# Attention layers of a hybrid backbone: the softmax division moved from the probabilities to the output, four value products to a PSUM bank

## The chip, the cores and the metric

The kernel runs on one core of one Trainium2 chip. The metric is the device time of one execution in microseconds (us); the time of a kernel is the median of its runs. A profile is one execution recorded by the hardware profiler. Its engines are PE (matrix unit; PEld is its weight load), DVE (vector), ACT (scalar), POOL (GpSimd) and SP, which issues the loads.

## The reference

Four layers work on 256 context tokens and 256 latent tokens of width 1024. Layers 0 and 3 mix tokens with windowed grouped-query attention (16 heads of 64, 4 key heads, a learned sink logit for each head; called the window layers here), layer 1 with multi-head latent attention (16 heads; the latent layer), layer 2 with a recurrence. A gated MLP follows each. What the change touches is the end of the attention:

```python
def attend(q, k, v, mask=None, sink=None):
    s = jnp.einsum("bqhgd,bkhd->bhgqk", q, k, preferred_element_type=jnp.float32) * (q.shape[-1] ** -0.5)
    if mask is not None:
        s = jnp.where(mask, s, NEG_INF)
    m = jnp.max(s, axis=-1)
    if sink is not None:
        sk = jnp.broadcast_to(sink.astype(jnp.float32)[None, :, :, None], m.shape)
        m = jnp.maximum(m, sk)
    p = jnp.exp(s - m[..., None])
    denom = jnp.sum(p, axis=-1)
    if sink is not None:
        denom = denom + jnp.exp(sk - m)
    o = jnp.einsum("bhgqk,bkhd->bqhgd", p, v.astype(jnp.float32))
    o = o / jnp.transpose(denom, (0, 3, 1, 2))[..., None]
    return o.astype(v.dtype)
```

The quotient may be taken before or after the product with v: the denominator belongs to a query row.

## The kernel before, in words

Activations lie transposed, 128 features to a tile. A weight unit of 128 x 1024 values is loaded by SP, rounded by ACT (`whi`, L214), and the rest of the rounding is taken by POOL (`wlo`, L215); a projection is three products of high and low parts (`mm3`, L224 to L226). The order of instructions on each engine is fixed when the program is built, by a scheduler that walks the program and fills an engine's gaps with later work; at run time each engine takes its own list in order.

A window layer (`swa`) projects keys, then queries, and then calls `core(p, b, j)` for one pair of heads and one block of 128 queries at a time: p is the half of the heads, b the query block (0 and 1 context, 2 and 3 latent), j the pair. Layer 0 makes 2 x 4 x 4 = 32 such calls, layer 3 (latent only) 2 x 2 x 4 = 16. In a call PE makes the scores into a bank of `mm` (L642, L643). For context DVE takes the maximum (L658 to L660), for latent a fused mask, scale and maximum (L669) and a sign change (L672). ACT takes the exponential with its row sum (L662, L673). Then the sink is added to the sum (DVE L675, ACT L676, DVE L677), the reciprocal taken (DVE L678), and the two halves of P are multiplied by it, one on DVE (L683), one on ACT (L681). PE transposes the scaled P (L691), ACT and DVE copy it (`pt`, L242, L244), PE multiplies it with v into a bank of `mo` (L697), and ACT and DVE write the result as high and low part into `o` (`split`, L258, L259), 128 columns at a time.

The latent layer (`mla`) does the same in `core(hg, hp, b)`, 4 x 2 x 4 = 32 calls, with scores L884, maximum L888 to L892, exponential L894, reciprocal L895, both scalings on DVE (L897), transposes L905 and value products L911. Between its calls the keys and queries of the next group of heads are prepared (`kv_put` and `q_mm`; transposes L834 and L858, which follow a chain of small DVE operations, L265 to L275 and `rqs`, L866).

PSUM pools have two banks each: `mm`, `fl`, `mo`, `tp`. In layer 0 the modulation vectors of the layer are computed alongside (`mod0_steps`, L339): one `mo` bank is held for a sum over 8 and then one over 16 weight tiles, one tile per call of `core`, so through most of layer 0 the attention has the other `mo` bank alone. While the second half of the heads is worked on, the output projection of the first half (`half_proj`, on `o`) is put between the calls; that of the second half (`out_tail`) follows the last call. In the window layers `o[p]` is read by these projections in four slices of j, in the latent layer in slices of (hg, hp).

## Time and profile before

| what | value |
|---|---|
| runs | 2292.27, 2292.8, 2296.81 us; median 2292.8 us |
| profiled execution, its own time | 2288.72 us |
| span of its profile, first to last instruction | 2286.9 us |
| busy: PE, DVE, ACT, POOL | 93%, 71%, 45%, 42% of the span |
| mean granted TensorE clock | 0.979 |
| chain that ended last | PE 73%, DVE 19%, ACT 4% |

The attention of layer 0 lies at about 97 to 275 us of the span, that of layer 1 at 733 to 922, that of layer 3 at 1985 to 2075. "Busy" of PE is the union of its matmuls' spans, so work that fills gaps between matmuls and work that runs back to back look alike in it. The list of waits gives, for each instruction that made its engine idle, what ended the wait. Where an engine's own list is in order, a late instruction delays all that stands behind it.

### The profile page before, as it was taken

The numbers are of one execution on the slowest core, as the hardware profiler recorded it, in microseconds if no ns is written. First come the engines' busy times: TensorE is split into PE (matmuls) and PEld (weight loads), VectorE is DVE, ScalarE is ACT, GpSimd is POOL, SyncE is SP. The second block draws the span as 40 slices with busy tenths as digits, with TensorE's granted clock in tenths as the row PEclk, the third lists the DMA queues.
The fourth block names the chain that finished last, engine by engine and source line by source line (L and its number), as shares of the span: only waits on it lengthen the run. The fifth ranks groups of instructions, "written<-read, shape, count | busy, mean of one in ns | idle before, by whom it ended". The sixth has DMA issues, their size and how long they took to land.

```text
span 2286.9 us, 32497 instructions
## 1 busy us (share of the span) xinstructions
PE 2133.3 (93%) x12084; PEld 1772.5 (78%) x12084; DVE 1628.4 (71%) x3342; ACT 1031.6 (45%) x1850; POOL 956.4 (42%) x418
## 2 busy tenths in 40 slices
PE   6989999999989998899999988899999999898999
PEld 5656788888877666888888876688888887677999
DVE  4678779777776887687879789857964457885333
ACT  4466553232246775433232356635333224575544
POOL 3231145454533002354545433344544443414887
PEclk9999999999999999999999998899999999999999
DMA  8433135555522001155556422223655552303555
GB/s 301 183 120 130 38 119 190 173 172 166 176 88 66 21 29 56 54 196 175 174 175 186 128 71 68 74 83 111 193 182 172 174 162 83 102 32 98 185 184 157
DMA packets 83884, 300.11 MB, mean 131 GB/s; under 512 B 11152, under 2 KB 12816, under 8 KB 81296
## 3 DMA queue, kind: packets, MB, share of 16 engines
q1 hardware_dynamic: 83728, 298.05, 40.2%
q8 instruction: 95, 1.56, 0.3%
q14 instruction: 61, 0.50, 0.1%
HBM read 296.97 MB, written 1.05 MB: 130 GB/s over the span
## 4 chain that ended last, share of the span: by engine, by line
PE 73%; DVE 19%; ACT 4%; issue 2%; DMA 2%; POOL 1%; SPq 0%; ACTq 0%; DVEq 0%; POOLq 0%
PE fl L225 8%; PE fl L226 8%; PE fl L224 8%; PE mm L224 7%; PE mm L226 7%; PE mm L225 7%; PE mo L225 4%; PE mo L224 4%; PE mo L226 4%; PE tp L226 2%; PE tp L224 2%; PE tp L225 2%; PE mo L697 2%; PE tp L691 2%; PE mm L884 2%
## 5 line engine op out<-in xcount | busy, mean ns | idle before, releaser
L215 POOL TENSOR_TENSOR wlo<-raw,whi 128x1024 fp32r<-128x1024 f32 (+3 forms) x367 | 922.4, 2516 | 1247.9 <-ACT whi L214 1212.4
L214 ACT ACTIVATE whi<-raw 128x1024 fp32r<-128x1024 f32 (+3 forms) x367 | 382.4, 1043 | 480.6 <-PE tp L225 189.9
L373 DVE SCALAR_TENSOR_TENSOR junk<-mw,cbc 128x1024 bf16<-128x1024 f32 x256 | 456.6, 1784 | 24.1 <-DMA mw<-in_modw_dram 15.8
L224 PE MATMUL fl<-h_hi,whi 128*128 128x512 f32 (+1 forms) x832 | 298.7, 360 | 10.4 <-DVE lam L958 5.9
L226 PE MATMUL fl<-h_hi,wlo 128*128 128x512 f32 (+1 forms) x832 | 298.9, 360 | 3.6 <-POOL wlo L215 3.6
L225 PE MATMUL fl<-h_lo,whi 128*128 128x512 f32 (+1 forms) x832 | 298.9, 360 | 0.4 <-POOL h_lo L439 0.2
L224 PE MATMUL mm<-h_hi,whi 128*128 128x512 f32 (+1 forms) x768 | 271.1, 353 | 3.1 <-ACT h_hi L435 2.7
L226 PE MATMUL mm<-h_hi,wlo 128*128 128x512 f32 (+1 forms) x768 | 270.1, 352 | 3.7 <-POOL wlo L215 3.7
L225 PE MATMUL mm<-h_lo,whi 128*128 128x512 f32 (+1 forms) x768 | 269.6, 352 | 0.8 <-POOL h_lo L439 0.2
L1109 DVE SCALAR_TENSOR_TENSOR conv<-mm,colt,conv 128x510 f32<-128x510 f32 (+1 forms) x88 | 59.8, 680 | 190.3 <-ACT conv L1107 190.3
L224 PEld LDWEIGHTS fl<-h_hi,whi 128*128 128x128 f32 x832 | 158.8, 192 | 34.2 <-issue 6.0
L1113 ACT ACTIVATE conv<-conv 128x512 f32<-128x512 f32 (+1 forms) x88 | 51.0, 580 | 287.4 <-DVE conv L1111 287.3
L226 PEld LDWEIGHTS fl<-h_hi,wlo 128*128 128x128 f32 x832 | 159.0, 191 | 27.2 <-POOL wlo L215 4.6
L225 PEld LDWEIGHTS fl<-h_lo,whi 128*128 128x128 f32 x832 | 159.1, 191 | 23.5 <-POOL h_lo L439 0.6
L224 PE MATMUL mo<-g_hi,whi 128*128 128x256 f32 (+1 forms) x488 | 165.4, 339 | 9.8 <-DVE x L449 6.8
L224 PEld LDWEIGHTS mm<-h_hi,whi 128*128 128x128 f32 x768 | 147.2, 192 | 23.3 <-ACT h_hi L435 3.7
L225 PE MATMUL mo<-g_lo,whi 128*128 128x256 f32 (+1 forms) x488 | 164.6, 337 | 0.4 <-DVE g_lo L259 0.4
L226 PEld LDWEIGHTS mm<-h_hi,wlo 128*128 128x128 f32 x768 | 146.8, 191 | 23.1 <-POOL wlo L215 4.3
L226 PE MATMUL mo<-g_hi,wlo 128*128 128x256 f32 (+1 forms) x488 | 164.4, 337 | 0.0
L225 PEld LDWEIGHTS mm<-h_lo,whi 128*128 128x128 f32 x768 | 146.3, 191 | 20.7 <-POOL h_lo L439 1.4
L449 DVE SCALAR_TENSOR_TENSOR x<-mo,modc,x 128x256 f32<-128x256 f32 x212 | 95.3, 477 | 84.2 <-PE mo L226 83.9
L224 PEld LDWEIGHTS mo<-g_hi,whi 128*128 128x128 f32 x488 | 93.1, 191 | 21.9 <-DVE x L449 7.5
(313 smaller groups left out, 4443.9 us busy)
## 6 DMA issues: line engine op xcount, KB each, us to landing
raw<-in_W_dram SPq DMA_DIRECT2D x352, 512.0 KB, 3.6
mw<-in_modw_dram SPq DMA_DIRECT2D x144, 512.0 KB, 4.2
mw<-in_modwa_dram SPq DMA_DIRECT2D x8, 1024.0 KB, 15.2
mw<-in_modwb_dram SPq DMA_DIRECT2D x16, 512.0 KB, 4.5
mw<-in_modwb_dram SPq DMA_DIRECT2D x8, 1024.0 KB, 8.6
cbc<-in_cc_dram SPq DMA_DIRECT2D x3, 1024.0 KB, 6.1
raw<-in_W_dram SPq DMA_DIRECT2D x8, 384.0 KB, 2.9
x<-in_xT_dram SPq DMA_DIRECT2D x8, 256.0 KB, 4.9
```

The source lines that it names most:

```text
L214: nc.scalar.activation(hi, raw, AF.Copy)
L215: nc.gpsimd.tensor_tensor(lo, raw, f32(hi), op=ALU.subtract)
L224: nc.tensor.matmul(ps, ah, bh, start=start and i == 0, stop=False, **kw)
L225: nc.tensor.matmul(ps, ah, bl, start=False, stop=False, **kw)
L226: op = nc.tensor.matmul(ps, al, bh, start=False, stop=stop and i == n - 1, **kw)
L373: nc.vector.scalar_tensor_tensor(junk, raw, 1.0, cbc[:, s], op0=ALU.mult, op1=ALU.mult, accum_out=modc[l][:, s, m:m + 1])
L449: nc.vector.scalar_tensor_tensor(X[m][:, half], ps[:, half], modc[l][:, s, part + m:part + m + 1], X[m][:, half], op0=ALU.mult, op1=ALU.add)
L691: nc.tensor.transpose(pp[:, c:c + 128], P[z][:, (2 * kp + kk) * 128:(2 * kp + kk + 1) * 128], ident)
L697: nc.tensor.matmul(po[r], v[0][:, kb, p * 128 + 64 * z:p * 128 + 64 * z + 64], pt[:, kp, (kk * 2 + z) * 128:(kk * 2 + z + 1) * 128], start ...
L884: nc.tensor.matmul(ps[:, c], d["q"][:96, 2 * hp + z, bc], d["k"][:96, 2 * hp + z, :nk], start=True, stop=True)
L1109: op = nc.vector.scalar_tensor_tensor(y3[:, :, 1:], g3[:, :, :255], cw[:, l, 0, f:f + 1], y3[:, :, 1:], op0=ALU.mult, op1=ALU.add)
L1113: nc.scalar.activation(y[:, t0:], y[:, t0:], AF.Silu)
```

## The change

A helper `divide` is new. Instead of scaling P, the kernel keeps the sums of the exponentials of four calls (the four j of a window layer's (p, b); the four b of a latent layer's (hg, hp)), collects the four value products in one bank of `mo`, and after the fourth takes the reciprocals of all eight sums at once, spreads them over 512 columns (ACT, `rw`), transposes that (PE, four transposes into `tp`), copies it (ACT, `rs`), multiplies the bank by it in place (DVE), and splits all 512 columns into `o`. In the window layers the latent scale `rqs` carries a minus sign, so that the fused operation gives the negated maximum at once and the sign change (L672) falls away; the sink terms are taken for eight columns at a time.

```diff
@@ -258,6 +258,19 @@
         nc.scalar.activation(hi, src, AF.Copy)
         nc.vector.tensor_tensor(lo, src, f32(hi), op=ALU.subtract)
 
+    def divide(po, rd, dst):
+        wide = tmp("rw")
+        nc.scalar.activation(wide.rearrange("p (m z d) -> p m z d", m=4, z=2),
+                             rd.rearrange("p m (z o) -> p m z o", o=1).to_broadcast([128, 4, 2, 64]), AF.Copy)
+        rb = tp_ps()
+        for m in range(4):
+            nc.tensor.transpose(rb[:, m * 128:(m + 1) * 128], wide[:, m * 128:(m + 1) * 128], ident)
+        rs = tmp("rs")
+        nc.scalar.activation(rs, rb, AF.Copy)
+        nc.vector.tensor_tensor(po, po, rs, op=ALU.mult)
+        view = po.rearrange("p (m q) -> p m q", m=4) if len(dst[0].shape) == 3 else po
+        split(dst[0], dst[1], view)
+
     def rsqrt(v, n, steps=3):
         i = small(n, "rs_i", I32)
         y = small(n, "rs_y")
@@ -634,7 +647,7 @@
                 else:
                     nc.vector.tensor_copy(qb[:, z], pq)
             rq = mean_rsqrt(ss, 8, 64)
-            nc.vector.tensor_scalar(rqs[p][:, b * 8:(b + 1) * 8], rq, 0.125, None, op0=ALU.mult)
+            nc.vector.tensor_scalar(rqs[p][:, b * 8:(b + 1) * 8], rq, 0.125 if b < 2 else -0.125, None, op0=ALU.mult)
 
         def scores(ps, p, b, j, g, nk):
             h = 2 * j + g
@@ -642,46 +655,42 @@
             nc.tensor.matmul(ps, q, kh[:, 2 * p + g, :nk], start=True, stop=False)
             nc.tensor.matmul(ps, q, kl[:, 2 * p + g, :nk], start=False, stop=True)
 
+        G = {}
+
         def core(p, b, j):
             if o[p] is None:
                 o[p] = bigs("o", 2)
+            if j == 0:
+                st = small(32, "st")
+                G[p, b] = [st[:, a * 8:(a + 1) * 8] for a in range(4)] + [mo_ps()]
+            ngm, es, den, rd, po = G[p, b]
             nk = 256 if b < 2 else 512
-            st = small(12, "st")
-            mx, ngm, es, den, rd = (st[:, a * 2:(a + 1) * 2] for a in range(5))
-            sk, nsk2 = (a.rearrange("p (k j) -> p j k", j=4)[:, j, 2 * p:2 * p + 2] for a in (snk, nsk))
+            nsk2 = nsk[:, 8 * p + j:8 * p + 8:4]
             rq2 = rqs[p][:, b * 8 + 2 * j:b * 8 + 2 * j + 2]
             P = []
             if b < 2:
                 ps, pt = mm_ps(), probs()
                 for z in range(2):
                     scores(ps[:, z * 256:(z + 1) * 256], p, b, j, z, nk)
+                mx = small(2, "mx")
                 nc.vector.tensor_reduce(mx, ps.rearrange("p (z k) -> p z k", z=2), axis=AX.X, op=ALU.max, negate=True)
                 nc.vector.tensor_tensor(mx, mx, rq2, op=ALU.mult)
-                nc.vector.tensor_tensor(ngm, mx, nsk2, op=ALU.min)
+                nc.vector.tensor_tensor(ngm[:, j::4], mx, nsk2, op=ALU.min)
                 for z in range(2):
+                    c = 4 * z + j
                     nc.scalar.activation(pt[:, z * 256:(z + 1) * 256], ps[:, z * 256:(z + 1) * 256], AF.Exp,
-                                         bias=ngm[:, z:z + 1], scale=rq2[:, z:z + 1], accum_out=den[:, z:z + 1])
+                                         bias=ngm[:, c:c + 1], scale=rq2[:, z:z + 1], accum_out=den[:, c:c + 1])
                     P.append(pt[:, z * 256:(z + 1) * 256])
             else:
                 for z in range(2):
+                    c = 4 * z + j
                     ps, pt = mm_ps(), probs()
                     scores(ps, p, b, j, z, nk)
                     nc.vector.tensor_tensor_reduce(
-                        out=pt, in0=ps, in1=mask[:, b - 2], op0=ALU.add, op1=ALU.max,
-                        scale=rq2[:, z:z + 1], scalar=sk[:, z:z + 1], accum_out=mx[:, z:z + 1])
-                    nc.vector.tensor_scalar(ngm[:, z:z + 1], mx[:, z:z + 1], -1.0, None, op0=ALU.mult)
-                    nc.scalar.activation(pt, pt, AF.Exp, bias=ngm[:, z:z + 1], accum_out=den[:, z:z + 1])
+                        out=pt, in0=ps, in1=mask[:, b - 2], op0=ALU.add, op1=ALU.min,
+                        scale=rq2[:, z:z + 1], scalar=nsk2[:, z:z + 1], accum_out=ngm[:, c:c + 1])
+                    nc.scalar.activation(pt, pt, AF.Exp, bias=ngm[:, c:c + 1], scale=-1.0, accum_out=den[:, c:c + 1])
                     P.append(pt)
-            nc.vector.tensor_tensor(es, sk, ngm, op=ALU.add)
-            nc.scalar.activation(es, es, AF.Exp)
-            nc.vector.tensor_tensor(den, den, es, op=ALU.add)
-            nc.vector.reciprocal(rd, den)
-            for z in range(2):
-                if z:
-                    nc.scalar.activation(P[z], P[z], AF.Copy, scale=rd[:, z:z + 1])
-                else:
-                    nc.vector.tensor_scalar(P[z], P[z], rd[:, z:z + 1], None, op0=ALU.mult)
-            po = mo_ps()[:, :128]
             pt = pt_p.tile([128, 2, T], F32, tag="pt", name="pt")
             for kp in range(nk // 256):
                 pp = tp_ps()
@@ -693,10 +702,15 @@
                 for kk in range(2):
                     kb = 2 * kp + kk
                     for z in range(2):
-                        r = slice(64 * z, 64 * z + 64)
-                        nc.tensor.matmul(po[r], v[0][:, kb, p * 128 + 64 * z:p * 128 + 64 * z + 64],
+                        nc.tensor.matmul(po[64 * z:64 * z + 64, j * 128:(j + 1) * 128], v[0][:, kb, p * 128 + 64 * z:p * 128 + 64 * z + 64],
                                          pt[:, kp, (kk * 2 + z) * 128:(kk * 2 + z + 1) * 128], start=kb == 0, stop=kb == nk // 128 - 1)
-            put(sel(o[p], slice(None), j, slice(b * 128, (b + 1) * 128)), po)
+            if j == 3:
+                nc.vector.tensor_tensor(es, snk[:, 8 * p:8 * p + 8], ngm, op=ALU.add)
+                nc.scalar.activation(es, es, AF.Exp)
+                nc.vector.tensor_tensor(den, den, es, op=ALU.add)
+                nc.vector.reciprocal(rd, den)
+                divide(po, rd.rearrange("p (z m) -> p m z", z=2),
+                       [t[:, :, b * 128:(b + 1) * 128] for t in o[p]])
 
         ps = {b: mm_ps() if z < 2 else fl_ps() for z, b in enumerate(range(q0, 4))}
         proj(1, ps, hook=lambda q, done: steps(mods, MQ[q]))
@@ -796,7 +810,7 @@
                     nc.vector.tensor_tensor(krg[:, b], kr, c32k[:, b - 2], op=ALU.mult)
                     nc.vector.tensor_tensor(krg[:, b], krg[:, b], r, op=ALU.add)
 
-        G, o, uq, ukv = {}, {}, {}, {}
+        G, o, uq, ukv, acc = {}, {}, {}, {}, {}
 
         def group(hg):
             G[hg] = dict(q=big("q", F32), k=big("k", F32), v=big("v", F32).rearrange("p b (c n) -> p b c n", c=2)[:, :, 0],
@@ -874,8 +888,12 @@
             nk = 512 if lat else 256
             bc = slice(b * 128, (b + 1) * 128)
             rq2 = d["rqs"][:, b * 4 + 2 * hp:b * 4 + 2 * hp + 2]
-            st = small(8, "st")
-            mx, ngm, den, rd = (st[:, a * 2:(a + 1) * 2] for a in range(4))
+            if b == 0:
+                acc[hg, hp] = small(16, "st"), mo_ps()
+            st, po = acc[hg, hp]
+            den, rd = st[:, 2 * b:2 * b + 2], st[:, 8:16]
+            st = small(4, "mx")
+            mx, ngm = st[:, 0:2], st[:, 2:4]
             P, S = [], []
             for z in range(2):
                 if z == 0 or lat:
@@ -892,10 +910,6 @@
                 nc.vector.tensor_tensor(ngm, mx, rq2, op=ALU.mult)
             for z in range(2):
                 nc.scalar.activation(P[z], S[z], AF.Exp, bias=ngm[:, z:z + 1], scale=rq2[:, z:z + 1], accum_out=den[:, z:z + 1])
-            nc.vector.reciprocal(rd, den)
-            for z in range(2):
-                nc.vector.tensor_scalar(P[z], P[z], rd[:, z:z + 1], None, op0=ALU.mult)
-            po = mo_ps()[:, :128]
             pt = pt_p.tile([128, 2, T], F32, tag="pt", name="pt")
             for kp in range(nk // 256):
                 pp = tp_ps()
@@ -908,9 +922,11 @@
                     kb = 2 * kp + kk
                     for z in range(2):
                         c = hp * 128 + 64 * z
-                        nc.tensor.matmul(po[64 * z:64 * z + 64], d["v"][:, kb, c:c + 64], pt[:, kp, (kk * 2 + z) * 128:(kk * 2 + z + 1) * 128],
+                        nc.tensor.matmul(po[64 * z:64 * z + 64, bc], d["v"][:, kb, c:c + 64], pt[:, kp, (kk * 2 + z) * 128:(kk * 2 + z + 1) * 128],
                                          start=kb == 0, stop=kb == nk // 128 - 1)
-            put(sel(o[hg // 2], slice(None), (2 * hg + hp) % 4, bc), po)
+            if b == 3:
+                nc.vector.reciprocal(rd, acc[hg, hp][0][:, 0:8])
+                divide(po, rd.rearrange("p (m z) -> p m z", z=2), [t[:, (2 * hg + hp) % 4] for t in o[hg // 2]])
 
         group(0)
         ss = small(16, "ssk")
```

How the scheduler's lists change is shown at three places.

PE, layer 0. `mo_<n>` names a bank's use and `o0_`/`o1_` the parts of `o`; rows with L642, L643 (L655, L656 in the new numbering) are scores, L691 (L700) transposes of P, L697 (L705) value products, L267 transposes of the reciprocals. Before, in the second half of layer 0, each call has its own `mo`:

```order
L697 MATMUL mo_2032<-pt_2033,v_613 64x128 x8
L691 MATMUL tp_2084<-tabt_104,P_2066 128x128 x4
L642 MATMUL mm_2200<-k_hi_653,q_1288 128x256
L643 MATMUL mm_2200<-k_lo_654,q_1288 128x256
L642 MATMUL mm_2200<-k_hi_653,q_1288 128x256
L691 MATMUL tp_2122<-tabt_104,P_2104 128x128
L224 MATMUL fl_2146<-o0_938,whi_2142 128x512
L225 MATMUL fl_2146<-o1_939,whi_2142 128x512
L697 MATMUL mo_2082<-pt_2083,v_613 64x128 x4
```

With the change, where the first group of layer 0 ends and the second begins:

```order
L705 MATMUL mo_941<-pt_1202,v_613 64x128 x4
L267 MATMUL tp_1219<-tabt_104,rw_1217 128x128 x4
L700 MATMUL tp_1248<-tabt_104,P_1236 128x128 x4
L655 MATMUL mm_1341<-k_hi_653,q_855 128x256
L656 MATMUL mm_1341<-k_lo_654,q_855 128x256
L655 MATMUL mm_1341<-k_hi_653,q_855 128x256
L656 MATMUL mm_1341<-k_lo_654,q_855 128x256
L705 MATMUL mo_1234<-pt_1247,v_613 64x128 x4
```

The four transposes of the reciprocals stand right behind the last value product of a group, and between them and the first product of the next group stand one transposed P and four scores.

PE, the end of layer 3's attention, where the last value products pass into the output projection of the second half of the heads (`o0_17456` before, `o0_17132` with the change). Before:

```order
L224 MATMUL fl_17960<-o0_17456,whi_17956 128x256
L225 MATMUL fl_17960<-o1_17457,whi_17956 128x256
L226 MATMUL fl_17960<-o0_17456,wlo_17957 128x256
L697 MATMUL mo_17916<-pt_17917,v_16670 64x128 x4
L226 MATMUL fl_17974<-o0_17456,wlo_17957 128x256
L697 MATMUL mo_17916<-pt_17917,v_16670 64x128 x4
L224 MATMUL fl_17974<-o0_17456,whi_17956 128x256
L225 MATMUL fl_17974<-o1_17457,whi_17956 128x256
L226 MATMUL fl_17974<-o0_17456,wlo_17957 128x256
```

With the change:

```order
L705 MATMUL mo_17353<-pt_17519,v_16406 64x128 x8
L267 MATMUL tp_17546<-tabt_104,rw_17544 128x128 x4
L224 MATMUL fl_17576<-o0_17132,whi_17572 128x256
L224 MATMUL fl_17590<-o0_17132,whi_17572 128x256
L225 MATMUL fl_17576<-o1_17133,whi_17572 128x256
L226 MATMUL fl_17576<-o0_17132,wlo_17573 128x256
```

Before, the projection of the earlier slices of j stands around the last value products; with the change nothing of the projection stands before the last division, since all four slices of the last block are written by it.

DVE, the last two latent calls of layer 3. Before (`st` holds the small row values, `x` is the projection's result):

```order
L669 ISA P,st<-mm,mask,rowt,rqs 128x512
L669 ISA st 128x1
L259 TENSOR_TENSOR o_17457<-mo,o_17456 128x128
L683 TENSOR_SCALAR P<-P,st 128x512
L672 TENSOR_SCALAR st<-st 128x1
L449 SCALAR_TENSOR_TENSOR x_101<-fl,modc_127,x_101 128x256
L675 TENSOR_TENSOR st<-rowt,st 128x2
L244 COPY pt<-tp 128x512
L677 TENSOR_TENSOR st<-st 128x2
L678 RECIPROCAL st<-st 128x2
L683 TENSOR_SCALAR P<-P,st 128x512
```

With the change:

```order
L689 ISA P,st<-mm,mask,nsk,rqs 128x512
L689 ISA st 128x1
L708 TENSOR_TENSOR st<-rowt,st 128x8
L710 TENSOR_TENSOR st<-st 128x8
L711 RECIPROCAL st<-st 128x8
L244 COPY pt<-tp 128x512
L462 SCALAR_TENSOR_TENSOR x_101<-fl,modc_127,x_101 128x256
L270 TENSOR_TENSOR mo<-mo,rs 128x512
L259 TENSOR_TENSOR o_17133<-mo,o_17132 128x4x128
```

Nothing of DVE stands between a latent call's exponential and its transposes any more; the sink, the reciprocal, the product (L270) and the low part follow once per group.

## Rows read from the trace of the kernel before

**Rows 1.** Busy time by stretch (start:end, us, PE, PEld, DVE, ACT, POOL, clock, DMA share, GB/s).
```profile
97.00:275.00 178.00, 160.88 (x1170) 110.87 (x1169) 139.47 (x482) 114.81 (x302) 30.04 (x14) 1.00 0.30 99
733.00:922.00 189.00, 171.24 (x1082) 122.66 (x1081) 145.09 (x495) 122.00 (x295) 27.16 (x13) 0.98 0.11 33
1985.00:2075.00 90.00, 80.44 (x643) 63.35 (x642) 76.36 (x266) 63.78 (x152) 19.17 (x8) 0.98 0.15 50
```
**Rows 2.** PE's waits in layer 0's stretch (us in total, times, longest).
```profile
PE tp L691 <- DVE P L683: 11.1, 6, 3.5
```
**Rows 3.** PE's waits in layer 1's stretch.
```profile
PE tp L834 <- DVE rqs L866: 9.7, 3, 4.0
```
**Rows 4.** PE's waits in layer 3's stretch.
```profile
PE tp L691 <- DVE P L683: 3.7, 4, 2.4
PE tp L691 <- DVE st L672: 2.3, 2, 1.7
```
**Rows 5.** Order of time at 243 to 248 us (start, us, instruction, [idle before <- releaser]).
```profile
244.05 2.36 POOL L215 TENSOR_TENSOR wlo<-raw,whi 128x1024 fp32r<-128x1024 f32 x1 [16.39 <-ACT whi L214]
244.19 2.51 DVE L683 TENSOR_SCALAR P<-P,st 128x512 f32<-128x512 f32 x1
...
246.85 1.06 PE L691 MATMUL tp<-tabt,P 128*128 128x128 f32 x8 [1.58 <-DVE P L683]
```
**Rows 6.** Order of time at 2004 to 2014 us, and the clock of that stretch.
```profile
2007.88 0.19 ACT L673 ACTIVATION_READ_ACCUMULATOR P<-P,st 128x1 f32 x1
...
2009.69 0.48 DVE L683 TENSOR_SCALAR P<-P,st 128x512 f32<-128x512 f32 x1
...
2010.32 1.94 PE L691 MATMUL tp<-tabt,P 128*128 128x128 f32 x8 [2.39 <-DVE P L683]
...
2005.00:2015.00 10.00, 7.61 (x67) 5.86 (x64) 8.58 (x29) 6.46 (x16) 2.38 (x1) 0.83 0.17 55
```
**Rows 7.** Groups that the change removes (count | busy us, mean ns | idle before).
```profile
L681 ACT ACTIVATE P<-P,st 128x512 f32<-128x512 f32 (+1 forms) x48 | 30.9, 646 | 16.1 <-DVE st L678 10.0 <-DVE st L672 2.2 <-DVE st L677 1.5
L897 DVE TENSOR_SCALAR P<-P,st 128x256 f32<-128x256 f32 (+1 forms) x64 | 26.3, 441 | 0.5
L683 DVE TENSOR_SCALAR P<-P,st 128x512 f32<-128x512 f32 (+1 forms) x48 | 25.6, 534 | 0.5
L259 DVE TENSOR_TENSOR o<-mo,o 128x128 fp32r<-128x128 f32 x80 | 23.1, 288 | 23.5 <-ACT o L258 22.8
L258 ACT ACTIVATE o<-mo 128x128 fp32r<-128x128 f32 x80 | 22.0, 275 | 27.6 <-PE mo L697 17.2 <-PE mo L911 9.5
L672 DVE TENSOR_SCALAR st<-st 128x1 f32<-128x1 f32 x64 | 8.5, 146 | 0.1
L895 DVE RECIPROCAL st<-st 128x2 f32<-128x2 f32 x32 | 5.2, 162 | 14.1 <-ACT P L894 14.1
```
**Rows 8.** Nearest to what it adds: by source line (min/median/max ns), and two groups by form.
```profile
L601 ACT ACTIVATE P<-kr x8: 614/630/631, 70.8 to 1969.7; 128x512 f32<-128x512 f32 x8
L242 ACT ACTIVATE pt<-tp x96: 575/597/632, 107.0 to 2066.1; 128x512 f32<-128x512 f32 x96
L1114 DVE TENSOR_TENSOR fl<-conv,fl 128x512 f32<-128x512 f32 x66 | 45.5, 690 | 16.0 <-PE fl L226 8.4 <-ACT conv L1113 7.6
L259 DVE TENSOR_TENSOR g_lo<-fl,g_hi 128x512 fp32r<-128x512 f32 x66 | 45.0, 682 | 8.1 <-ACT g_hi L258 8.1
```
**Rows 9.** The chain of waits near 106 us (start, us, what).
```profile
106.49 0.44 PE tp L691 x4
```
**Rows 10.** The latent layer's transposes of P as a group.
```profile
L905 PE MATMUL tp<-tabt,P 128*128 128x128 f32 x192 | 28.6, 276 | 1.6 <-DVE P L897 1.6
```
**Rows 11.** Two scores behind each other in layer 0, order of time.
```profile
198.47 0.28 PE L643 MATMUL mm<-k_lo,q 128*128 128x256 f32 x1
198.59 0.28 PE L642 MATMUL mm<-k_hi,q 128*128 128x256 f32 x1
```
**Rows 12.** The window layers' value products as a group.
```profile
L697 PE MATMUL mo<-pt,v 128*64 128x128 f32 x640 | 49.4, 285 | 0.4 <-ACT pt L242 0.2
```

## The prediction, made before the changed kernel ran

> **What bounds the kernel now.** I read the page first: PE is busy for 93% of the span and makes up 73% of the chain that ended last, so a change in the attention counts for as much as it changes PE's idle time or PE's work. Then the busy time by stretch, to see the three attention stages apart [rows 1]: the reader is to see there that PE is idle for 178.00 - 160.88 = 17.1 us in layer 0, 17.8 us in layer 1 and 9.6 us in layer 3, together 44.5 us, and that DVE, at 139.5, 145.1 and 76.4 us (361.0 us, 79% of the stretches), is the next busiest engine and well ahead of ACT. Then PE's waits in each stretch. In layer 0 most of the idle time, 11.1 us in six waits, is spent on a P that DVE has not yet scaled [rows 2]; in layer 3 it is 3.7 us on the same and 2.3 us where the sign change came last [rows 4]; in layer 1 the scaled P costs only 1.6 us [rows 10], and the largest wait, 9.7 us in three pieces, is for the norm chain of the next group's queries and keys, which DVE also makes [rows 3]. Last the order of time around such waits. In one, DVE's scaling takes 2.51 us, against a mean of 534 ns, while a POOL instruction of 2.36 us runs beside it, and PE stands for 1.58 us [rows 5, 7]. In another the exponential's sum is out at 2008.07 us and the transposes begin only at 2010.32, because sink, reciprocal and scaling wait their turn in DVE's list; PE stands 2.39 us, and the granted clock of those 10 us is 0.83, so that eight transposes take 1.94 us instead of 1.06 [rows 5, 6].
>
> **What it removes.** From DVE the two scalings, 25.6 and 26.3 us, the 80 small low-part writes, 23.1 us, and five groups of small operations of 5.2 to 8.5 us (sign change, sink, sum, two reciprocals), 37.5 us: 112.5 us [rows 7]. From ACT the other scaling, 30.9 us, and 80 high-part writes, 22.0 us [rows 7], with some small exponentials.
>
> **What it adds, for each of 20 groups** (8, 8 and 4 in the three layers). On ACT the spread, at the 630 ns of a broadcast copy of that size, and a copy and a high part, at 595 ns each: 1.82 us, 36.4 us in all [rows 8]. On DVE the product at 690 ns and the low part at 682 ns, 1.37 us, 27.4 us in all [rows 8], and 44 small operations at some 0.16 us, a reciprocal's mean [rows 7], 7 us. Net, DVE's list gets 78 us lighter, over a fifth of its 361 us, and ACT's about 16 us. On PE four transposes, 80 in all; four behind each other take 0.44 us [rows 9]: 8.8 us. If they fill time in which PE is idle anyway, half of that, 4.4; if each costs what the latent layer's transposes cost as a group, 28.6 us over 192 [rows 10], it is 11.9 us. I take 8.8, since PE is the engine that is mostly busy.
>
> **What that does on the path.**
> 1. *The waits for a scaled P end.* The transposes now need only the exponential. In the one case that was done long before [rows 5], in the other some 2.2 of 2.39 us lie behind it [rows 6]. Of the 11.1 + 3.7 + 1.6 = 16.4 us I take 14 as gone, and 1 of the 2.3 us behind the sign change: -15 us. What is late next there is the exponential itself, behind DVE's maximum, which can still be held up; if each wait falls only by the undisturbed length of the removed chain (a small exponential, two small operations, a scaling: about 1 us), 8 us go. Ends: -8 to -18.7.
> 2. *The clock.* The dip costs 10 x (1 - 0.83) = 1.7 us [rows 6]; without the wait I take -1.5. Ends: 0 and -3.
> 3. *The other waits.* 44.5 - 18.7 = 25.8 us of PE idle remain, much of it behind chains on DVE that are still there [rows 3]. With DVE's list a fifth lighter I take a third, -8. No row shows what a lighter list does; the ends are 0 (the chains keep their length and their hold-ups) and -16 (two thirds).
> 4. *PE's own new work*: +8.8 (above).
> 5. *Handing the bank over.* From the end of the reciprocals' transposes to a free bank it takes copy, product, high and low part: 0.595 + 0.690 + 0.595 + 0.682 = 2.6 us [rows 8]. In layer 0 the modulation sums hold the other `mo` bank, so at four group ends the next group's first value product must wait for that. At the first, the list gives PE four transposes and four scores in between, 0.44 + 4 x 0.12 = 0.9 us [rows 9, 11], so PE waits 1.7 us; at the others I count 3.3, 2.8 and 2.2 us of such work, so 0.4 more. +2. In layers 1 and 3 the second bank is free: nothing. Ends: 0 and 4 x 2.6 = 10.4.
> 6. *The last division.* In the order of layer 3's end nothing stands between the last transposes and the output projection, which needs the whole block: +2.6, against no wait there before. In layer 0 five matmuls of 512 columns stand in between (0.23 us each, twice the 0.12 of 256 columns [rows 11]): +1.4. In layer 1 nine: +0.5. Together +4.5; ends 0 and 7.8. Behind the waiting projection stand all its further matmuls.
>
> The small operations on DVE and ACT and the longer evacuations themselves I cost at nothing: they lie beside PE's work, in lists that get lighter; without that cover, an ACT list that had to carry them alone would cost their 36 us.
>
> **A rule weighed.** Before, PE waited only 0.4 us in all in front of 640 value products, although in layer 0 one bank had to serve call after call [rows 12]: each 128-column evacuation, 275 + 288 ns [rows 7], was hidden. The Trainium skill, page "Perfetto Trace Analysis", section "Matmuls", says that independent matmul groups should rotate through different PSUM banks, so that evacuating one overlaps the next group's matmuls; collecting four products in a bank goes against it. If every hand-over of layer 0 and every last division stood open, terms 5 and 6 would be 18.2 instead of 6.5 us; that is the slower rival below.
>
> **Sum.** -15 - 1.5 - 8 + 8.8 + 2 + 4.5 = -9.2 us. The profiled execution before took 2288.72 us, its span is 2286.9; with the change it would take 2279.5. The median of the runs shown is 4.1 us above that execution, so I predict 2283.6, say 2284 us.
>
> **The rivals.** A measurement of this kernel can tell about 0.2%, 4.6 us, from no change.
> - *DVE set the pace throughout.* If the lighter list lets PE run through, a quarter of the 44.5 us idle remains: -33.4 - 1.5 + 8.8 + 6.5 = -20, 2273 us. For it: DVE at 79% beside a PE that waits almost only for DVE. Against: layer 1's waits are for another chain [rows 3]. Chance 0.2.
> - *No gain: the wait moves on.* POOL's hold-ups [rows 5] strike the next DVE operation in line (a maximum's small operations), so term 1 is -11 and term 3 -3: -11 - 1.5 - 3 + 15.3 = 0, 2293 us. Chance 0.22.
> - *Slower: the bank hand-over.* In layer 0 and at each layer's end the 2.6 us of item 5 stand open because PE's list has reached the next group's first product before the bank is free: 7 x 2.6 = 18.2. With terms 1, 2 and 4 as they are and no term 3 it gives -15 - 1.5 + 8.8 + 18.2 = +10.5, 2303 us. It decides from 16.5 - 8.8 = 7.7 us on, which is three open hand-overs. For it: layer 3's end and the first group's end are laid out so. Against: at three of the four in layer 0 other work stands between. This is the case that the rule above describes. Chance 0.16.
> - The forecast itself: 0.42, with 2277 to 2288 us as its own range.
>
> **The numbers.** Faster by over 0.2% (below 2288.2): 0.42 + 0.2 = 0.62. Within: 0.22. Slower: 0.16. The range must reach into the cases on both sides: down to 2267 (the first rival with a part of its terms at their lower ends) and up to 2299 (the last one with two of its seven hand-overs covered). I leave out 0.06 below and 0.12 above.
>
> **What would show it.** Right: PE's waits for P drop below 4 us over the three stretches and end on ACT's exponential; DVE's busy time there falls from 361 to about 283 us, ACT's by about 16; each new group of four transposes adds 0.44 us; a wait of 2 to 3 us stands ahead of layer 3's output projection, and one of 1 to 2 us ahead of the second group of layer 0; the clock of layer 3 has no dip at 0.83. Wrong: PE's idle time in the stretches stays above 40 us, or waits in front of value products (now 0.4 us) sum to more than 8 us; or a stretch outside the attention changes by more than 2 us, which no step here provides for.

## The result: 1.5% slower, and the profile after

The changed kernel takes 2326.85 us (median of 4 runs, 2325.09 to 2332.11) against 2293.05 us before: a ratio of 1.0148, 95% interval 1.0128 to 1.0168. The prediction was 2284 us, and its range ended at 2299. The profiled execution took 2332.11 us, its span is 2330.2 us; before, it was 2286.9. The one is the slowest of its kernel's runs and the other (2288.72 us) the fastest, so the two profiles differ by 43.3 us where the medians differ by 33.8.

First the busy time by stretch, with the same work in each line as in [rows 1] (start:end, length, then PE, PEld, DVE, ACT, POOL, the granted clock, DMA share, GB/s), and a line of 6.5 us out of the second:

```profile
96.50:274.50 178.00, 165.97 (x1203) 116.65 (x1202) 111.29 (x331) 102.62 (x237) 30.28 (x14) 0.99 0.32 104
732.40:950.20 217.80, 183.45 (x1114) 129.74 (x1113) 124.73 (x391) 128.79 (x289) 27.21 (x13) 0.94 0.10 29
2022.00:2117.80 95.80, 83.82 (x660) 65.85 (x659) 65.26 (x175) 55.98 (x120) 19.04 (x8) 0.96 0.17 46
893.00:899.50 6.50, 5.61 (x16) 4.54 (x17) 4.30 (x10) 2.31 (x4) 2.13 (x1) 0.50 0.20 76
```

Layer 0 keeps its 178 us, the latent layer grows from 189.0 to 217.8, layer 3 from 90.0 to 95.8: 34.6 us together, about the loss of the medians. The other 8.7 us of the profile lie outside these stretches, nearly all between layer 1 and layer 3, where the code is that of before; from the last product of layer 1's output projection to layer 3's last spread of keys the traces take 1023.9 us (before) to 1034.6 us (`l0_only`), 1032.8 after. Each layer can be taken apart into PE's idle time (length minus PE), four transposes a group at 0.44 us [rows 9], and the clock (length times what the clock lacks of 1.00; an upper bound to the rounding of the clock, since PE is idle for part of it):

| us more than before | idle | transposes | clock, at most | sum | grown by |
|---|---|---|---|---|---|
| layer 0 | 12.0 - 17.1 = -5.1 | 3.5 | 1.8 - 0 | 0.2 | 0 |
| layer 1 (latent) | 34.4 - 17.8 = +16.6 | 3.5 | 13.1 - 3.8 | 29.4 | 28.8 |
| layer 3 | 12.0 - 9.6 = +2.4 | 1.8 | 3.8 - 1.8 | 6.2 | 5.8 |

PE's waits (us in total, times, longest), the largest of layer 0, then of layer 1 ([rows 2, 3] before):

```profile
PE mo L352 <- DMA mw<-in_modwb_dram: 5.6, 5, 1.5
PE mo L705 <- DVE o L259: 2.1, 1, 2.1
PE fl L224 <- ACT o L258: 1.5, 1, 1.5
PE tp L700 <- ACT P L681: 1.2, 3, 0.6
```
```profile
PE tp L848 <- DVE rqs L880: 16.2, 5, 5.1
PE fl L224 <- ACT v L831: 6.8, 3, 2.7
PE tp L919 <- ACT P L912: 5.3, 8, 1.8
```

The waits for a scaled P are gone: 11.1 us in layer 0 have become 1.2 us behind the exponential. In layer 0 PE only comes earlier to what is late next, the modulation's weights (5.6 us, 2.8 before) and the bank. In layer 1 there was little of this kind to gain (1.6 us), and three waits have grown: for the norm chain of the next keys (16.2 against 9.7 us), for P, now behind the exponential (5.3 us), and, new, for `v`, that is for a bank that the preparation of the next heads needs empty.

Why, is seen in order of time at one group's end in layer 1, ACT's part first (start, us, instruction, [idle before <- releaser]):

```profile
856.94 0.63 ACT L263 ACTIVATE rw<-st 128x512 f32<-128x512 f32 x1 [0.27 <-DVE st L928]
857.48 1.06 ACT L242 ACTIVATE pt<-tp 128x512 f32<-128x512 f32 x2
860.11 0.60 ACT L269 ACTIVATE rs<-tp 128x512 f32<-128x512 f32 x1 [1.57 <-PE tp L267]
860.60 0.47 ACT L830 ACTIVATE kraw<-fl,mrr 128x256 f32<-128x256 f32 x1
860.96 0.58 ACT L859 ACTIVATE sq<-fl,mrr 128x384 f32<-128x384 f32 x1
...
862.20 0.49 ACT L831 ACTIVATE v<-fl,mrr 128x256 f32<-128x256 f32 x1
```
```profile
858.39 1.09 PE L925 MATMUL mo<-pt,v 128*64 128x128 f32 x16
859.41 0.66 PE L267 MATMUL tp<-tabt,rw 128*128 128x128 f32 x4
862.75 0.80 PE L224 MATMUL fl<-whi,ck_hl 128*128 128x512 f32 x1 [2.68 <-ACT v L831]
```
```profile
860.74 0.70 DVE L270 TENSOR_TENSOR mo<-mo,rs 128x512 f32<-128x512 f32 x1 [3.83 <-ACT rs L269]
861.57 0.55 DVE L860 TENSOR_REDUCE ss<-sq 128x4 f32<-128x384 f32 x1
862.04 0.41 DVE L834 TENSOR_REDUCE ss<-kraw 128x4 f32<-128x256 f32 x1
```

The division is a round trip over three engines: ACT spreads the reciprocals (`rw`), PE transposes them behind the last value products, ACT copies them (`rs`), DVE multiplies. Each engine works its list in order. ACT stands 1.57 us before `rs`, and the copies that empty the `fl` banks stand behind it; DVE stands 3.83 us before its multiplication, and the sums of the norm chain stand behind that; PE stands 2.68 us. At this group's end it is ACT's list that holds the sums too: they read `sq` and `kraw`, which ACT makes behind `rs`, and L860 starts 0.03 us after `sq` is out (860.96 + 0.58). Over the program, all three layers (count | busy, mean ns | idle before):

```profile
L270 DVE TENSOR_TENSOR mo<-mo,rs 128x512 f32<-128x512 f32 x20 | 14.0, 699 | 47.8 <-ACT rs L269 42.2 <-ACT kraw L830 5.2 <-PE mo L705 0.4
L267 PE MATMUL tp<-tabt,rw 128*128 128x128 f32 x80 | 13.5, 285 | 0.0
L269 ACT ACTIVATE rs<-tp 128x512 f32<-128x512 f32 x20 | 11.9, 596 | 23.3 <-PE tp L267 23.2
```

In layer 1's stretch alone DVE stands 30.3 us before its eight products and ACT 10.2 us before its eight copies.

And the idle time is paid again. After a wait of 5.07 us the clock stood at half (the stretch of 893.00 above shows 0.50, 1.2 instead of 2.4 GHz), and matmuls of 512 columns start 0.43 us apart, against 0.23 at 884.08 and 884.31, where the clock is 1.00:

```profile
888.48 0.34 PE L226 MATMUL fl<-whi,cq_lo 128*128 128x384 f32 x1
893.89 1.06 PE L848 MATMUL tp<-tabt,kn 128*96 128x128 f32 x4 [5.07 <-DVE rqs L880]
...
895.17 0.63 PE L225 MATMUL fl<-o,whi 128*128 128x512 f32 x1
895.60 0.63 PE L226 MATMUL fl<-o,wlo 128*128 128x512 f32 x1
```

Not all of this wait is the division's. In the norm chain ahead of it two operations on 128 x 8 values take over 2 us, while a `wlo` of POOL runs beside each (886.62 to 889.00 and 889.52 to 891.86 us); the same operations take 0.17 us elsewhere in the chain:

```profile
886.67 2.36 DVE L278 TENSOR_SCALAR rs_i<-rs_v 128x8 int32<-128x8 int32 x1
889.67 2.20 DVE L283 SCALAR_TENSOR_TENSOR rs_y<-rs_t,rs_y 128x8 f32<-128x8 f32 x1
```

Such hold-ups do not explain the loss: in layer 1's stretch DVE's order of time has 10 rows of over 1.2 us before and 8 after.

### The profile page after: what moved, and what is told of

Read it like the earlier page. It is cut to its first block, busy times and chain, and to the rows that moved or that the text cites. A ratio compares the mean times of both kernels' runs of the same rounds, so it can differ in the third digit from the quotient of the medians.

```text
span 2330.2 us, 32212 instructions
## 1 busy us (share of the span) xinstructions
PE 2155.4 (92%) x12164; PEld 1789.0 (77%) x12164; DVE 1572.6 (67%) x2994; ACT 1017.4 (44%) x1746; POOL 958.5 (41%) x418
## 3 DMA queue, kind: packets, MB, share of 16 engines
q8 instruction: 96, 1.57, 0.3%
```

## The experiments

The diffs are abridged. Theory A: in the latent layer the division's round trip holds the in-order lists of ACT and DVE, PE idles, and the clock falls. Every ratio is to the kernel before, with its 95% interval. "Layer 1" is the trace's stretch of [rows 1] with the same work (189.0 us before), "layer 3 on" the time from the last spread of the keys to the end of the span (before: 2286.9 - 1969.7 = 317.2 us [rows 8]; after: 2330.2 - 2006.8 = 323.4).

**1 and 2. One layer kind each.** `win_only` has the change in the window layers alone, `lat_only` in the latent layer alone; the other layers are word for word as before. The first:

```diff
 def core(hg, hp, b):
+    nc.vector.reciprocal(rd, den)
+    nc.vector.tensor_scalar(P[z], P[z], rd[:, z:z + 1], None, op0=ALU.mult)
-    divide(po, ...)
```

> Division behind the value products in the two window layers only; the latent layer divides the probabilities as before. Theory A (the loss arises in the latent layer, where the 28.8 us more of its stretch is PE idling behind the division's round trip and the half clock that follows): the latent layer's stretch returns to about 227 us and the time to 2293 - 0.7 + 6.2 = about 2299 us (2294 to 2303). Theory B (the loss is general, e.g. code or clock of the whole program, and only shows up in layer 1): over 2312 us.

> The change in the latent layer alone; the window layers divide the probabilities as before. Theory A: 2293 + 29 = about 2322 us (2316 to 2327), and with the run of the window layers alone the two differences add up to the 34 us of the whole change within 4 us. Theory B: under 2312 us.

`win_only` took 2300.9 us (1.0027, 1.0013 to 1.0041), `lat_only` 2332.5 us (1.0161, 1.0135 to 1.0187). The loss is the latent layer's: theory B falls. The differences, 7 and 39 us, do not add up to 34 within 4 us as expected, and `lat_only` lies above its range: it scatters from 2322 to 2334.5 us, and in its profile layer 0, whose code is that of before, is itself 7 us longer, which stays open. The layer itself is clear. From its first score to the last product of its output projection it takes 216.0 us before and 215.9 in `win_only`, 244.8 after and 244.9 in `lat_only`.

**3. The division written later.** Only its place in the latent layer's program moves.

```diff
 def core(hg, hp, b):
-    if b == 3: reciprocal; divide(po, ...)
...
     for b in MP[h] if hg < 3 else ():
         kv_mm; q_mm; mean_rsqrt; kv_put; q_scale
+    if h % 2: close(hg, h // 2)      # reciprocal; divide
```

> The whole change, but in the latent layer the division of a finished bank is written behind the key and query preparation of that step, so that the copies that free the preparation's banks stand ahead of the wait for the transposed reciprocals in ScalarE's list. Theory A (in-order lists of ScalarE and VectorE are held by the round trip reciprocal spread, transposes, copy, multiplication): PE's waits for v and for the key norm in the latent stretch fall from 23 us to under 12 us, the stretch by 12 to 20 us, time 2306 to 2316 us. Theory C (the collection itself is the cost: one bank for four products, wide outputs that come late, four more transposes): the stretch changes by less than 5 us, time 2322 to 2330 us.

2299.63 us (1.003, 1.0017 to 1.0044): 27 us of the 34 come back, more than theory A asked (2306 to 2316). Layer 1 by stretch, PE's largest waits in it, and ACT's list at a group's end:

```profile
730.50:924.20 193.70, 176.16 (x1121) 126.75 (x1120) 127.49 (x394) 127.47 (x288) 27.30 (x13) 0.97 0.12 34
```
```profile
PE tp L848 <- DVE rqs L880: 9.4, 5, 3.2
PE tp L919 <- ACT P L912: 2.7, 2, 1.5
```
```profile
839.92 0.63 ACT L263 ACTIVATE rw<-st 128x512 f32<-128x512 f32 x1
840.44 0.57 ACT L912 ACTIVATE P<-mm,mx,rqs 128x256 f32<-128x256 f32 x1
...
842.76 0.60 ACT L849 ACTIVATE k<-tp 96x512 f32<-96x512 f32 x1
843.62 0.60 ACT L269 ACTIVATE rs<-tp 128x512 f32<-128x512 f32 x1 [0.26 <-PE tp L267]
```

Between `rw` and `rs` ACT now has three exponentials and two copies to do, and stands 0.26 instead of 1.57 us. The waits for `v` are gone, idle time is 17.5 us as before (17.8). 4.7 us of the layer are left by these stretches, 3.9 (219.9 against 216.0) from the first score to the last product of the projection.

**4. No division at all** in the latent layer (it is left out, the products are only collected and written out).

```diff
-    divide(po, ...)
+    split(*[t[:, (2 * hg + hp) % 4] for t in o[hg // 2]], po)
```

> The whole change, but in the latent layer the collected bank is written out without any division: no reciprocal, no spread, no transposes of it, no copy, no multiplication; that part of the computation is left out. Theory A: the latent stretch falls by 20 to 30 us, time 2297 to 2307 us. Theory C: the collection stays and with it most of the loss, time over 2318 us.

2302.51 us (1.0045, 1.003 to 1.0059). Collecting four products in a bank costs the latent layer little (its stretch is 192.5 us, PE idle for 18.2 of it), so theory C falls; and written later, the division is nearly as cheap as none (219.9 against 219.0 us by the longer measure). What `lat_late` leaves is therefore not simply its transposes: without them most of it stays. Nor does the wait for the norm chain follow the division alone, since it is 12.6 us here, with a longest of 5.1; the wait for `v` is gone in both.

**5. Another engine for the copy.**

```diff
-    nc.scalar.activation(rs, rb, AF.Copy)
+    nc.vector.tensor_copy(rs, rb)        # in the latent layer
```

> The whole change, but in the latent layer VectorE instead of ScalarE copies the transposed reciprocals out of PSUM. Theory A1 (ScalarE's list, in which the copies that free the preparation's banks stand behind that copy, is what counts): PE's 6.8 us of waits for v go, and with them about half of the 16.6 us of idle time and some of the half clock, 2306 to 2318 us. Theory A2 (VectorE's list counts, the multiplication at whose head everything waits): less than 5 us off, 2322 to 2328 us.

2321.84 us (1.0118, 1.0103 to 1.0133), between the ranges of A1 and A2: 5 us back, and still 5.1 us of waits for `v` and 10.8 for the norm chain. The run does not free ACT's list, so it cannot part A1 from A2. DVE now waits for the transposes itself (24.8 us in the layer, before `rs`), and ACT stands 8.7 us before `o`, its copy of the divided bank, with `v` behind it: at 859.51 us `o` starts after 1.95 us of idle time, `v` at 860.01, and PE has stood 2.57 us. Another engine for the copy moves the hold; another place for the trip, as in `lat_late`, takes most of it away.

**6 to 9. Layer 3.** The same remedy there, the layer undone, the collection alone, and, in the kernel before, only the order in which the output projection adds its four products. `l3_late` and `l3_old` start from `lat_late`, the other two from the kernel before:

```diff
 l3_late, in layer 3:
-    if j == 3: es, den, rd; divide(po, ...)
+    if j == 3: done.append((p, b))
...
     core(*c)
+    if c[2] != 3: close()
```
```diff
 l3_old, in layer 3:
+    P[z] *= rd[:, z]
-    if j == 3: es, den, rd; divide(po, ...)
+    put(sel(o[p], slice(None), j, ...), po)
```
```diff
 l3_collect, in layer 3 of the kernel before:
-    put(sel(o[p], slice(None), j, ...), po)
+    if j == 3: put(sel(o[p], slice(None), slice(None), ...), G[p, b])
```
```diff
 l3_rev, in layer 3 of the kernel before:
-    proj_cols(..., for k in range(4)], src, ...)
+    proj_cols(..., for k in (3, 2, 1, 0)], [src[k] for k in (3, 2, 1, 0)], ...)
```

> As the run with the later latent division (2299.6 us), and in layer 3 the division of a finished bank is written behind the next call's scores and value products. Theory H (the held lists of VectorE and ScalarE cost layer 3 its 6 us, as in the latent layer): 2293 to 2296 us, PE's longest wait in the layer, 4.4 us for a query's low half, under 2.5 us. Theory F (the output projection of the first heads is PE's cover work and can begin only when all four products of a bank are divided): no gain, 2298 to 2302 us.

> As the run with the later latent division (2299.6 us), but the second window layer divides the probabilities again, call by call (with the sign carried into the exponential's scale). Layer 3 added 6 to 7 us in every run that has the change there; theory A says that this is the layer's own and comes back: 2293 us (2290 to 2296). A rival, that a later stretch passes on what an earlier one lost, leaves 2298 or more.

> The kernel before, in layer 3 alone the four products of divided probabilities are collected in one bank and written out together after the fourth call; nothing else changes, no transposes of reciprocals. Theory F: 4 to 7 us slower than before, 2297 to 2300 us, the first output projection of the layer some 15 us later. Theory H: 2291 to 2295 us.

> The kernel before, but the output projection of layer 3's first four heads adds its four products in the reverse order, the last head first; attention itself is untouched. Theory F (what the collection takes from layer 3 is the early start of this projection as cover for PE's waits): the first projection product moves from 2016 us to about 2032 us, layer 3 grows by 3 to 6 us, 2296.5 to 2300 us. Theory G (the collecting bank, its wide copies or its hand-over cost it): 2292 to 2295 us, as before.

| | us | ratio | layer 3 on, us | first projection product after the keys' spread, us |
|---|---|---|---|---|
| before | | 1 | 317.2 | 46.2 |
| after | 2326.85 | 1.0148 | 323.4 | 65.4 |
| l3_late | 2300.04 | 1.0025 (1.0014 to 1.0036) | 323.1 | 67.9 |
| l3_old | 2297.3 | 1.0014 (1.0003 to 1.0024) | 319.8 | 45.1 |
| l3_collect | 2299.36 | 1.0021 (1.001 to 1.0031) | 321.8 | 63.9 |
| l3_rev | 2301.17 | 1.0029 (1.002 to 1.0039) | 324.7 | 63.7 |
| lat_only, layer 3 as before | 2332.5 | 1.0161 | 316.3 | 45.0 |
| l0_only, layer 3 as before | 2296.4 | 0.9992 | 319.0 | 47.2 |
| sign_only, the sign alone in layer 3 | 2293.24 | 0.9995 | 321.4 | 45.6 |

The last column comes from rows like these, of before, after and `l3_rev` (with 1969.7, 2006.8 and 1977.0 for the spread):

```profile
2015.87 0.28 PE L224 MATMUL fl<-o,whi 128*128 128x256 f32 x1
```
```profile
2072.16 0.39 PE L224 MATMUL fl<-o,whi 128*128 128x256 f32 x1 [0.23 <-ACT o L258]
```
```profile
2040.66 0.50 PE L224 MATMUL fl<-o,whi 128*128 128x256 f32 x2
```

The last two columns are one profiled execution each. With the code of before, layer 3 on takes 316.3 to 319.0 us, and `sign_only` shows 321.4 with an early start and no loss in its median, so the fourth column tells little below some 4 us. The two starts (45 to 47 and 64 to 68 us) are clear, and so is the time of `l3_rev` over its 12 runs (4.6 to 8.9 us slower).

Writing the division later gains nothing here (theory H falls): PE's longest wait in the layer, for a query's low half, stays; after and `l3_late`:

```profile
PE tp L644 <- DVE qhl L641: 4.4, 1, 4.4
```
```profile
PE tp L644 <- DVE qhl L641: 6.9, 2, 4.9
```

What holds that low half is open. `l3_rev` leaves the attention as it was and only lets the projection begin with the last pair of heads: it starts 17.5 us later and costs as much as layer 3 loses (7.6 us, against 7.4 for both window layers in `win_only`), a little more than theory F's range. Before, a pair's output is ready by itself, and the projection's first products fill PE's waits while the attention still runs; a collected bank gives all four pairs at once, after the eighth call instead of the fifth. `l3_old` came back less far than expected (2293) and lies between its two ranges; its 3.5 us may be what `lat_late` leaves in layer 1, but layer 3 on is 2.6 us longer too, so this is not shown. In layer 0 the projection starts later as well (at 202.2 instead of 187.7 us), without a loss that shows.

**10 to 12. Layer 0 and the sign.** `l0_new` and `l0_only` have the change in layer 0 alone, the first with the sign carried in layer 3 too; `sign_only` carries the sign in both window layers and divides P.

```diff
-    op1=ALU.max, scalar=sk; ngm = -mx; exp(pt, bias=ngm)
+    op1=ALU.min, scalar=nsk2; exp(pt, bias=ngm, scale=-1.0)     # rqs negated
```

> The change in layer 0 alone; the latent layer as before, layer 3 as before with the sign carried in the exponential's scale (no sign change between maximum and exponential). From the stretches of the runs so far, layer 0 gives between -0.4 and -2.7 us; the sign at most -2. Theory A: 2288 to 2293 us, and the idle before the transposes of the probabilities of layer 0 (11 us) shows up as 3.5 us of transposes, waits for the modulation's weights and one step of half clock. A rival, that layer 0's gain was real and only hidden by chance: under 2286 us.

> The change in layer 0 alone; the latent layer and layer 3 word for word as before. If what the traces of six runs show of layer 0 (-0.4 to -2.7 us) is all, 2291 to 2294 us, no difference that can be told. If the prediction's terms for layer 0 hold (11.1 us of waits gone, 3.5 us of transposes, 3 us of ends), 2284 to 2288 us.

> The sign alone: in both window layers the minimum of the negated scores is taken and the exponential gets a scale of -1, so that the 48 sign changes of the maximum on VectorE go; the division stays on the probabilities. Prediction's reading: PE's 2.3 us of waits for that line go, 2290 to 2292.5 us. Reading from layer 3 of the two earlier runs: the wait moves to the scaling behind it and other places, 2294 to 2298 us.

`l0_new` 2296.69 us (1.0012, 0.9999 to 1.0025), `l0_only` 2296.4 us (0.9992, 0.9977 to 1.0007; its runs of before had a median of 2296.26), `sign_only` 2293.24 us (0.9995, 0.9985 to 1.0005). The runs of before beside `l0_new` had a median of 2293.77, those beside `sign_only` the same 2296.26. None can be told from before: layer 0's 11 us of waits are worth at most 5.3 us by the interval of `l0_only`, the sign changes (64 of them [rows 7], not 48) at most 3.4. `l0_new` lies above both of its ranges; a hidden gain of layer 0 (under 2286) falls.

**13 and 14. Dividing without a round trip.** In the kernel before, the reciprocals scale the identity, and P is multiplied by it instead of scaled and transposed.

```diff
-    P[z] *= rd[:, z]                               # 128 x 256 or 512
+    dg[:, z] = ident * rd[:, z]                    # 128 x 128
-    nc.tensor.transpose(pp[:, c:c + 128], P[z][:, ...], ident)
+    nc.tensor.matmul(pp[:, c:c + 128], P[z][:, ...], dg[:, z * 128:(z + 1) * 128], ...)
```

> The kernel before, with the division folded into the transposes of the window layers: the identity is scaled by the reciprocals (128 x 128 a head) and P is multiplied by it instead of being scaled (128 x 256 or 512 a head) and then transposed. No collection, no round trip. What the first theory of the prediction had right (PE waits for the scaled P in the window layers, 14.8 us) would show here without the cost of collecting: each of the waits shortens by the difference of the two scalings, some 0.15 to 0.3 us a call and more where VectorE is behind, 2286 to 2292 us. Rival: what is late next (VectorE's other work, the weights of the modulation) takes it, 2292 to 2296 us.

> The same in the latent layer too: 64 scalings of 128 x 256 or 512 become 64 of 128 x 128. There PE waits little for P (1.6 us), so the theory expects no more than 1 to 2 us beyond the window layers alone, 2284 to 2292 us; rival: 2292 to 2297 us.

2337.42 us (1.0184, 1.0169 to 1.02) and 2374.76 us (1.0348, 1.0332 to 1.0363). The group of the transposes before, and what stands in its place in `win_diag`:

```profile
L691 PE MATMUL tp<-tabt,P 128*128 128x128 f32 x320 | 48.0, 281 | 18.0 <-DVE P L683 14.9 <-DVE st L672 2.3 <-DVE rs_y L270 0.3
```
```profile
L692 PE MATMUL tp<-dg,P 128*128 128x128 f32 x640 | 88.7, 286 | 9.3 <-DVE dg L684 4.3 <-ACT dg L682 2.8 <-DVE st L675 1.3
```

The waits halve as meant (18.0 to 9.3 us), but a product of these types is two instructions where a transpose is one: 40.7 us more PE time, nearly the whole loss of 43.8. Both runs lie far outside their ranges, in which this work of PE does not stand. The Trainium skill, page "Perfetto Trace Analysis", section "Transposes", asks that logical transposes use the transpose and not a standard matmul; these rows agree. No version that was run is clearly faster than the kernel before.

## Why the prediction was wrong, by its own steps

- **Term 1, the waits for P (-15).** Right as to the window layers' waits: 18.0 us before their transposes became 1.2 us, on ACT's exponential as foretold. In layer 1 the wait for P grew instead, from 1.6 to 5.3 us, so the sum over the three stretches is 6.5 us and not below 4. Wrong as to the time: `l0_only` shows no gain that can be told. Of layer 0's 11.1 us some 6 went to the weights, the bank and the projection, 3.5 to transposes, up to 1.8 to the clock.
- **Term 3, the other waits (-8), and the sentence that costs the small operations on DVE and ACT at nothing, "in lists that get lighter".** This is the step that failed. The lists did get lighter: DVE's busy time in the stretches fell from 361.0 to 301.3 us (the forecast was 283), ACT's by 13. But the lists were held by a wait, not by their load: in layer 1, 30.3 us of DVE and 10.2 us of ACT stood idle at the division, with the next heads' preparation behind them, and the layer's PE idle time rose by 16.6 us, where term 3 had 8 less over all. `lat_late` gives the same instructions another place: DVE and ACT stand 11.7 and 3.8 us there, and PE's idle time is back at 17.5 us. The prediction priced the trip only from the transposes to the free bank, 2.6 us, and only for PE; from `rw` to the product's end it takes 860.74 + 0.70 - 856.94 = 4.5 us, and it did not ask who stands behind `rs` and the product on their engines.
- **Term 2, the clock (-1.5).** Wrong in sign: some 13 us more went to the half clock over the three stretches, 9.3 of them in layer 1, where `lat_late` brings the clock from 0.94 back to 0.97. Layer 3 still dips (0.96 over its stretch).
- **Term 4, the transposes (+8.8).** Four behind each other take 0.60 to 0.66 us with their end, 13.5 us of busy time in all. At full clock the next instruction starts 0.44 us after the first of them (881.68 to 882.12 us), as the term had it, and the layers' sums agree.
- **Terms 5 and 6, bank and last division (+2, +4.5).** Nearly right: one wait of 2.1 us for the bank, one of 1.5 us behind layer 0, one of 2.0 us in layer 3, none behind layer 1. So the slower rival, open hand-overs of the bank, did not come about: value products waited 4.3 us in all. The time was slower by another mechanism.
- **Left out altogether:** the start of the first half's projection in layer 3. Four pairs' outputs now come at once; that takes PE's cover work. A start as late costs 4.6 to 8.9 us in `l3_rev`, without any of the other edits.
- **The bounds.** "Wrong" was to be PE's idle time above 40 us: it is 58.4. A stretch outside attention was to change by at most 2 us; between layers 1 and 3 it is 8.9 us, with the code unchanged. Why stays open: `win_only` and `l0_only`, whose latent layer is that of before, are 7.0 and 10.7 us longer there, `lat_late` 1.2.

## What to carry to other kernels

When an operation becomes a round trip over engines, list for every engine on the way what stands behind its waiting instruction; write the trip's second half behind independent work, as the 27 us of `lat_late` show. A result that is collected before it is passed on also starts its consumer later, and the consumer may be what filled the gaps (in layer 3 here, not in layer 0). A wait that goes is worth only what is not late next, and idle TensorE time can count for more than its length, as in layer 1.

## What the hardware showed beyond the forecast

Short idle stretches can cost the clock too: in layer 1, 16.6 us more idle time came with the mean clock at 0.94 instead of 0.98, some 9 us, and a wait of 5.07 us was followed by 6.5 us at 0.50. The sum of idle time does not decide it: in layer 0 it fell by 5.1 us, and the clock went from 1.00 to 0.99. A product of 128 x 128 by these types takes two instructions against a transpose's one (640 and 320, 88.7 and 48.0 us).
